# Two edits in the odd layer of a decoder trunk: normed heads without their softmax sums, and a mask added on another engine

## The chip, the core and the metric

The kernel runs on one core of a Trainium2 chip. A core has a tensor engine (TensorE, PE in the profile) whose weight loads (PEld) run ahead of its matmuls, a vector engine (VectorE, DVE), a scalar engine (ScalarE, ACT), GpSimd (POOL), and SyncE (SP), which here issues nearly all DMAs. Each engine takes its instructions in order and waits for the others by semaphores. Matmuls write to PSUM; the other data lie in SBUF. The metric is device time in microseconds (us), the median of several runs.

## The reference

Two layers on 1024 tokens of width 1024. The odd layer runs four differential heads (two attention maps, one subtracted from the other, then an RMS norm over the head's 128 outputs) beside eight forgetting heads (a causal softmax with a bias per key):

```python
def rmsnorm(x, g):
    y = x * lax.rsqrt(jnp.mean(x * x, axis=-1, keepdims=True) + NORM_EPS)
    return y * g

def diff_attention(q1, q2, k1, k2, v, lam):          # per block of 128 queries
    p = softmax(s1, axis=-1) - lam * softmax(s2, axis=-1)
    return einsum('bhqk,bkhe->bqhe', p, v)

def forgetting_attention(q, k, v, fcum):
    s = einsum('bqhd,bkhd->bhqk', q, k) * scale
    s = s + fcum[query] - fcum[key]
    s = where(causal_mask, s, -1e30)
    return einsum('bhqk,bkhd->bqhd', softmax(s, axis=-1), v)

o_d = rmsnorm(diff_attention(...), subln) * (1.0 - lam_init)
o = concatenate([o_d, forgetting_attention(...)]) * silu(z_gate)
return o @ w_out
```

## The kernel before

Activations lie with features on the 128 partitions and tokens along the free axis, in two halves of 512 tokens. Float32 accuracy comes from splitting each operand into a high and a low part, so a projection is three matmuls (L127, L128, L130). The odd layer's attention is woven with its projections: `weave` takes turns between the main work (attention of units 0 to 3, the differential heads, then 4 to 7, two forgetting heads each) and the filling work (projections of the next unit, and at the end the first half of the output product). A scheduler then orders each engine's instructions when the program is built; that order is fixed on the chip.

For each block `i` of 128 queries, `scores` writes a row of n = 128 (i + 1) scores into the one PSUM tile S of 1024 columns (L442). `soft` then makes one pass on VectorE (L464) that adds a bias or mask, scales, writes P and gives each query's minimum of the negated scores, read out by a second short instruction; ScalarE takes the exponential with that minimum as bias and the sum as by-product (L466). TensorE turns blocks of P (L501), the turned blocks are split into pt_h (ScalarE, L91) and pt_l (VectorE, L92), and the products with V follow (L510, L511, for differential heads L515 to L517) into a PSUM tile o.

The forgetting heads get their causal mask on TensorE: `scores` with `causal=True` closes each row with a bf16 product of an identity and the 128x128 mask (L446) into the row's last 128 columns. Their bias f, one row of 1024 keys broadcast to all partitions, is loaded per head by SP (L1009) into a tile x8 and added in `soft`.

In a differential head, P1 + (-lam l1 / l2) P2 is formed from the unnormalised maps (L945), so o is l1 times too large, where l1 is the first map's sum for each query. `to_rows` takes the reciprocals of four blocks' l1 (L475), transposes them on VectorE (L476), and writes them to memory in four small DMAs (L479); `step` loads them back broadcast (L958). `done` multiplies o by them on VectorE (L963) and squares the result on ScalarE (L964). `later` calls `rstd`, which sums the squares on TensorE (L205), adds EPS to the mean (L207), takes the reciprocal root by a bit trick and three Newton steps on VectorE, and spreads it again with TensorE (L217); L968 to L970 scale, gate (on GpSimd) and store.

GpSimd otherwise makes the low parts of weights (L92), which wait for ScalarE's high parts, the rope products (L348), the gates' share of the forgetting heads' sums (L492), and clears small tiles for `to_rows` (L474). Temporary tiles of 128x512 share eight buffers under the tag `t`.

Of the kernel before, what the change touches and what calls it, by code (L numbers as in the profile page):

```python
# [21 lines left out]
EPS = 1e-6  # L22
# [11 lines left out]
class Trunk:  # L34
# [161 lines left out]

    def rstd(self, s, n, col=None):
# [43 lines left out]
    def setup2(self):  # L241
# [7 lines left out]
        nc.vector.tensor_copy(self.smask, tri[:, :256])  # L249
        self.identb = self.const("identb", [128, 128], BF16)  # L250
        nc.vector.tensor_copy(self.identb, self.ident)
        self.nsink = self.const("nsink", [128, 8])
# [173 lines left out]

    def scores(self, qs, ks, i, keys, S, causal=False):

# [6 lines left out]
        while k0 < k1:  # L435
# [3 lines left out]
            dst = S[:, o:o + w]  # L439
            more = causal and e == k1  # L440
            for n, (a, k) in enumerate(zip(q, ks[k0 // 4])):
                nc.tensor.matmul(dst, a, k[:, s], start=(n == 0), stop=(n == len(q) - 1 and not more))  # L442
            o += w
            k0 = e
            if more:
                nc.tensor.matmul(S[:, o - 128:o], self.identb, self.mask[:, 896:], start=False, stop=True)  # L446

# [12 lines left out]
    def soft(self, S, n, add, scale, P, l, init=BIG):  # L460

        nc = self.nc
        nm = self.small()
        nc.vector.tensor_tensor_reduce(out=P[:, :n], in0=S[:, :n], in1=add, scale=-scale, scalar=init,  # L464
                                       op0=ALU.add, op1=ALU.min, accum_out=nm)
        nc.scalar.activation(P[:, :n], P[:, :n], AF.Exp, bias=nm, scale=-1.0, accum_out=l)  # L466
# [455 lines left out]
    def diff_items(self, u, st):  # L922
        nc = self.nc
        for c in range(2):
            o, L, steps = [], self.small(4), []
            for j in (2 * c, 2 * c + 1):
# [3 lines left out]

                def s_op(e, i, m, c=c, Ps=Ps, maps=maps, S_=S_, P_=P_, L=L, steps=steps):
                    n = 128 * (i + 1)
# [8 lines left out]
                    else:  # L941
# [19 lines left out]
                def done(c=c, o=o, steps=steps):  # L961
                    z, s = self.tmp(), self.tmp()
                    nc.vector.tensor_tensor(out=z, in0=o[0], in1=steps[0], op=ALU.mult)  # L963
                    nc.scalar.activation(s, z, AF.Square)  # L964

                    def later():
                        r = self.rstd(s, 128)
                        nc.vector.scalar_tensor_tensor(out=z, in0=z, scalar=self.subl, in1=r, op0=ALU.mult, op1=ALU.mult)  # L968
# [6 lines left out]
                        for e, i in enumerate((2 * j, 2 * j + 1)) for m in range(2)],  # L975
                       self.causal_groups(j, Ps, get, self.pv128, 0.162, lambda: st["V"], 0, step if j % 2 else None),
                       done if j % 2 else None, 1, 1 / 16.5)
# [25 lines left out]
    def forget_items(self, u, st):  # L1003
# [7 lines left out]
        for c in range(2):  # L1011
            for hh in range(2):
                def scores(i, S, hh=hh):
                    self.scores([a[hh] for a in st["q"][:i // 4 + 1]], [a[hh] for a in st["k"][:i // 4 + 1]], i,
                                (0, i + 1), causal=True, S=S)

                def done(o, c=c, hh=hh):
                    self.finish64(o, hh, st["g"][c], (1, u, c))
                    return ("mark", "odd0") if (u, c, hh) == (7, 0, 1) else None

                yield from self.causal_items(c, hh, scores, 0.108, lambda n, f=fb[hh]: f[:, :n], SC64, lambda: st["V"], done,
                                             1 / 26, (1, u, c), st["g"][c])
# [415 lines left out]
```

## Time and profile before

| | |
|---|---|
| median of 3 runs | 1376.84 us (1373.97 to 1377.67) |
| the profiled execution | 1375.71 us |
| its span, first to last instruction | 1373.9 us |
| mean granted TensorE clock | 0.989 |
| the first 690 us (the even layer and what lies before it) | TensorE busy 628.4 us, VectorE 490.9, ScalarE 381.1, GpSimd 185.8 |
| 715 to 860 us (most of the differential heads) | TensorE busy 135.9 of 145 us |

A row of a group reads: line, engine, operation, tile written <- tiles read, shapes, count | busy us, mean ns of one | idle us of the engine just before, and what ended it. A row of the timeline reads: start, duration, the instruction, and in brackets idle time before it. The durations of matmuls are modelled to their end and overlap, so two starts tell more of TensorE's pace than one duration. In names, `S` is the score tile, `p` the softmax numerators, `pj` a projection's sum, `wr` a raw weight and `wh`, `wl` its parts, `sm` small columns of statistics, `x` (x8) the bias f, `t` a temporary.

### The profile page before, as it was taken

The numbers are of one execution on the slowest core, as the hardware profiler recorded it, in microseconds if no ns is written. First come the engines' busy times: TensorE is split into PE (matmuls) and PEld (weight loads), VectorE is DVE, ScalarE is ACT, GpSimd is POOL, SyncE is SP. The second block draws the span as 40 slices with busy tenths as digits, with TensorE's granted clock in tenths as the row PEclk, the third lists the DMA queues.
The fourth block names the chain that finished last, engine by engine and source line by source line (L and its number), as shares of the span: only waits on it lengthen the run. The fifth ranks groups of instructions, "written<-read, shape, count | busy, mean of one in ns | idle before, by whom it ended". The sixth has DMA issues, their size and how long they took to land.

```text
span 1373.9 us, 20797 instructions
## 1 busy us (share of the span) xinstructions
PE 1274.9 (93%) x6940; PEld 1056.0 (77%) x6940; DVE 905.0 (66%) x1963; ACT 732.0 (53%) x1507; POOL 333.4 (24%) x316
## 2 busy tenths in 40 slices
PE   2899999999999999899889999999999999999996
PEld 1678778888777777778767777787888888887885
DVE  5855767777767775787877775767645554555475
ACT  4253226666457677854546554546445555556642
POOL 2243421421332215300103232321212111113400
PEclk9899999999999999999999999999999999999998
DMA  8706685555444543472623221212212121233283
GB/s 281 250 17 211 201 274 190 171 171 157 127 151 135 162 131 116 131 230 100 194 87 94 77 80 54 70 51 86 62 35 81 49 76 54 85 108 116 77 268 116
DMA packets 105132, 175.98 MB, mean 128 GB/s; under 512 B 16688, under 2 KB 25904, under 8 KB 105024
## 3 DMA queue, kind: packets, MB, share of 16 engines
q1 hardware_dynamic: 100512, 172.03, 39.5%
q10 hardware_dynamic: 4512, 2.62, 0.6%
q8 instruction: 54, 0.88, 0.3%
q14 instruction: 54, 0.44, 0.1%
HBM read 131.45 MB, written 31.74 MB: 119 GB/s over the span
## 4 chain that ended last, share of the span: by engine, by line
PE 54%; DVE 19%; DMA 9%; issue 8%; ACT 7%; SPq 2%; POOL 1%; DVEq 0%; POOLq 0%; ACTq 0%
PE pj L127 9%; PE pj L128 9%; PE pj L130 9%; PE S L442 7%; PE pt L501 4%; PE o L511 2%; DMA wr<-in_wout_dram 2%; DVE p L464 2%; PE S L127 2%; PE o L510 2%; PE S L130 2%; PE S L128 2%; DVE pt_l L92 2%; ACT p L466 1%; DVE t L347 1%
## 5 line engine op out<-in xcount | busy, mean ns | idle before, releaser
L127 PE MATMUL pj<-h,wh 128*128 128x512 f32 (+1 forms) x816 | 341.0, 418 | 2.0 <-ACT wh L91 2.0
L128 PE MATMUL pj<-h,wh 128*128 128x512 f32 (+1 forms) x816 | 322.2, 395 | 0.0
L130 PE MATMUL pj<-h,wl 128*128 128x512 f32 (+1 forms) x800 | 315.9, 395 | 1.6 <-DVE wl L92 1.6
L92 POOL TENSOR_TENSOR wl<-wr,wh 128x512 fp32r<-128x512 f32 x126 | 165.4, 1322 | 473.6 <-ACT wh L91 429.0
L466 ACT ACTIVATE p<-p,sm 128x128 f32<-128x128 f32 (+3 forms) x192 | 148.8, 775 | 140.4 <-DVE sm L464 137.9
L92 DVE TENSOR_TENSOR pt_l<-pt,pt_h 128x512 fp32r<-128x512 f32 (+1 forms) x232 | 147.0, 635 | 107.7 <-ACT pt_h L91 106.0
L442 PE MATMUL S<-qk,qk 96*128 96x512 f32 (+5 forms) x720 | 174.7, 344 | 21.5 <-DVE sm L464 12.4
L91 ACT ACTIVATE pt_h<-pt 128x512 fp32r<-128x512 f32 (+1 forms) x232 | 127.7, 552 | 100.3 <-PE pt L501 97.2
L130 PEld LDWEIGHTS pj<-h,wl 128*128 128x128 f32 x800 | 151.0, 189 | 34.0 <-DVE wl L92 3.1
L127 PEld LDWEIGHTS pj<-h,wh 128*128 128x128 f32 (+1 forms) x816 | 154.3, 189 | 20.1 <-ACT wh L91 2.9
L442 PEld LDWEIGHTS S<-qk,qk 128*128 128x128 f32 (+1 forms) x720 | 120.6, 189 | 63.4 <-DVE sm L464 27.7
L128 PEld LDWEIGHTS pj<-h,wh 128*128 128x128 f32 (+1 forms) x816 | 154.3, 189 | 16.6 <-DVE h L92 0.2
L91 ACT ACTIVATE wh<-wr 128x512 fp32r<-128x512 f32 x165 | 101.3, 622 | 118.4 <-PE S L128 38.7
L501 PE MATMUL pt<-ident,p 128*128 128x128 f32 x840 | 134.3, 275 | 3.7 <-DVE p L945 2.8
L501 PEld LDWEIGHTS pt<-ident,p 128*128 128x128 f32 x840 | 101.1, 140 | 27.0 <-DVE p L945 4.4
L464 DVE CUSTOM_DVE_ANT_0 p<-S,mask 128x640 f32<-128x640 f32 (+7 forms) x128 | 96.0, 750 | 33.8 <-PE S L442 33.0
L510 PE MATMUL o<-pt_h,v 128*128 128x256 f32 (+1 forms) x408 | 106.6, 281 | 1.5 <-ACT pt_h L91 1.0
L511 PE MATMUL o<-pt_l,v 128*128 128x256 f32 (+1 forms) x408 | 102.6, 286 | 5.5 <-DVE pt_l L92 5.1
L348 POOL TENSOR_TENSOR t<-t,rs 128x512 f32<-128x512 f32 x26 | 36.5, 1402 | 238.5 <-DMA t<-t 159.6
L511 PEld LDWEIGHTS o<-pt_l,v 128*128 128x128 f32 x408 | 77.3, 189 | 15.7 <-DVE pt_l L92 10.3
L510 PEld LDWEIGHTS o<-pt_h,v 128*128 128x128 f32 x408 | 77.2, 189 | 9.6 <-ACT pt_h L91 3.4
L464 DVE CUSTOM_DVE_ANT_0 p<-S,x 128x128 f32<-128x128 f32 (+3 forms) x64 | 48.2, 753 | 25.2 <-PE S L446 21.9
(315 smaller groups left out, 2284.7 us busy)
## 6 DMA issues: line engine op xcount, KB each, us to landing
wr<-in_wod_dram SPq DMA_DIRECT2D x80, 256.0 KB
wr<-in_wout_dram SPq DMA_DIRECT2D x68, 256.0 KB
ad<-in_wadab_dram SPq DMA_DIRECT2D x41, 256.0 KB
wr<-in_wev_dram SPq DMA_DIRECT2D x38, 256.0 KB
raw<-in_wadaa_dram SPq DMA_DIRECT2D x32, 256.0 KB
ogd<-t SPq DMA_DIRECT2D x32, 256.0 KB
t<-t SPq DMA_DIRECT2D x106, 64.0 KB
t<-rd SPq DMA_DIRECT2D x48, 128.0 KB
```

What stands on the lines that cost most here:

```text
L91: nc.scalar.activation(hi, src, AF.Copy)
L92: (lo_eng or nc.vector).tensor_tensor(out=lo, in0=src, in1=hi.bitcast(F32), op=ALU.subtract)
L127: nc.tensor.matmul(p, w[0][:, k, :m], h[0], start=first, stop=False)
L128: nc.tensor.matmul(p, w[0][:, k, :m], h[1], start=False, stop=last and w[1] is None)
L130: nc.tensor.matmul(p, w[1][:, k, :m], h[0], start=False, stop=last)
L348: nc.gpsimd.tensor_tensor(out=s, in0=s, in1=self.rs[:, cs], op=ALU.mult)
L442: nc.tensor.matmul(dst, a, k[:, s], start=(n == 0), stop=(n == len(q) - 1 and not more))
L464: nc.vector.tensor_tensor_reduce(out=P[:, :n], in0=S[:, :n], in1=add, scale=-scale, scalar=init, op0=ALU.add, op1=ALU.min, accum_out=nm)
L466: nc.scalar.activation(P[:, :n], P[:, :n], AF.Exp, bias=nm, scale=-1.0, accum_out=l)
L501: nc.tensor.transpose(pt[:, n * 128:n * 128 + 128], b, self.ident)
L510: nc.tensor.matmul(o[:, qcols], w, hi[:, cols], start=start, stop=False)
L511: nc.tensor.matmul(o[:, qcols], w, lo[:, cols], start=False, stop=stop)
```

## The change

Two edits. First, a differential head's o stays unnormalised: with o' = l1 o, the norm o / sqrt(mean(o^2) + EPS) equals o' / sqrt(mean(o'^2) + EPS l1^2), so `rstd` takes EPS l1^2 (one small operation on the column of sums) in place of EPS, and `to_rows`, its DMAs and the multiplication of o go. ScalarE copies o out of PSUM and squares it. Second, the mask product goes; for each forgetting head and half GpSimd adds the mask to the 512 bias columns of that half's diagonal blocks (a tile W of tag `t`), and `soft` makes two passes: the first n - 128 columns with f, then the last 128 with W, starting from the first pass's minimum.

```diff
-        nc.vector.tensor_scalar(v, p[:, :nb], 1.0 / n, EPS, op0=ALU.mult, op1=ALU.add)
+        if eps is None:
+            nc.vector.tensor_scalar(v, p[:, :nb], 1.0 / n, EPS, op0=ALU.mult, op1=ALU.add)
+        else:
+            nc.vector.scalar_tensor_tensor(out=v, in0=p[:, :nb], scalar=1.0 / n, in1=eps, op0=ALU.mult, op1=ALU.add)
...
-            if more:
-                nc.tensor.matmul(S[:, o - 128:o], self.identb, self.mask[:, 896:], start=False, stop=True)
...
-        nm = self.small()
-        nc.vector.tensor_tensor_reduce(out=P[:, :n], in0=S[:, :n], in1=add, scale=-scale, scalar=init,
-                                       op0=ALU.add, op1=ALU.min, accum_out=nm)
+        k = 0
+        for a in add if isinstance(add, list) else [add]:
+            nm, s = self.small(), slice(k, k + a.shape[-1])
+            nc.vector.tensor_tensor_reduce(out=P[:, s], in0=S[:, s], in1=a, scale=-scale, scalar=init,
+                                           op0=ALU.add, op1=ALU.min, accum_out=nm)
+            init, k = nm, s.stop
...
-                        if i % 4 == 3:
-                            self.to_rows(L, self.rd[1, u, c, 0])
...
-                def step(c=c, steps=steps):
-                    t = self.tmp()
-                    nc.sync.dma_start(t, self.rd[1, u, c, 0:1, :].to_broadcast([128, C]))
-                    steps.append(t)
...
-                    nc.vector.tensor_tensor(out=z, in0=o[0], in1=steps[0], op=ALU.mult)
-                    nc.scalar.activation(s, z, AF.Square)
+                    nc.scalar.activation(z, o[0], AF.Copy)
+                    nc.scalar.activation(s, o[0], AF.Square)
+                    nc.vector.scalar_tensor_tensor(out=L, in0=L, scalar=EPS, in1=L, op0=ALU.mult, op1=ALU.mult)
...
-                        r = self.rstd(s, 128)
+                        r = self.rstd(s, 128, eps=L)
...
+                W = self.tmp()
+                tri = self.mask[:, 896:].rearrange("p (o k) -> p o k", o=1).to_broadcast([128, 4, 128])
+                nc.gpsimd.tensor_tensor(out=W.rearrange("p (b k) -> p b k", b=4), in1=tri, op=ALU.add,
+                                        in0=fb[hh][:, c * C:c * C + C].rearrange("p (b k) -> p b k", b=4))
+
+                def add(n, f=fb[hh], W=W, c=c):
+                    d = W[:, n - 128 - c * C:n - c * C]
+                    return [f[:, :n - 128], d] if n > 128 else d
...
-                                (0, i + 1), causal=True, S=S)
+                                (0, i + 1), S=S)
```

The order changes from the first differential head's finish on. Line numbers after the change are shifted by up to four in the code before `forget_items`; L463 is L464 of before, L441 is L442.

TensorE in unit 4, second half, first head (block 4, 640 columns: a 512-wide and a 128-wide piece of S). Before:

```order
L442 MATMUL S_10567<-qk_9919,qk_9730 128x128
L501 MATMUL pt_10556<-ident,p_10426 128x128 x3
L442 MATMUL S_10567<-qk_6995,qk_9730 128x128
L446 LDWEIGHTS identb
L446 MATMUL S_10567<-mask,identb 128x128
L127 MATMUL pj_10536<-h_7243,wh_10241 128x512
L128 MATMUL pj_10536<-h_7244,wh_10241 128x512
```

After:

```order
L441 MATMUL S_10503<-qk_9853,qk_9673 128x128
L441 MATMUL S_10503<-qk_6993,qk_9673 128x128
L127 MATMUL pj_10470<-h_7241,wh_10168 128x512
L501 MATMUL pt_10492<-ident,p_10357 128x128 x3
L128 MATMUL pj_10470<-h_7242,wh_10168 128x512
```

The load of the identity and the mask product are gone, and three turns moved behind the score row.

VectorE at the same place, the softmax of blocks 4 and 5. Before:

```order
L92 TENSOR_TENSOR pt_l_10545<-pt_10540,pt_h_10544 128x384
L464 ISA p_10568,sm_10574<-S_10567,x_2172_10215 128x640
L464 ISA sm_10574 128x1
L92 TENSOR_TENSOR pt_l_10561<-pt_10556,pt_h_10560 128x384
L464 ISA p_10584,sm_10590<-S_10583,x_2172_10215 128x768
L464 ISA sm_10590 128x1
```

After:

```order
L463 ISA p_10504,sm_10509<-S_10503,x_2157_10142 128x512
L463 ISA sm_10509 128x1
L92 TENSOR_TENSOR pt_l_10479<-pt_10474,pt_h_10478 128x384
L92 TENSOR_TENSOR pt_l_10497<-pt_10492,pt_h_10496 128x384
L463 ISA p_10504,sm_10511<-S_10503,t_10489,sm_10509 128x128
L463 ISA sm_10511 128x1
L463 ISA p_10521,sm_10526<-S_10520,x_2157_10142 128x640
L463 ISA sm_10526 128x1
L463 ISA p_10521,sm_10528<-S_10520,t_10489,sm_10526 128x128
L463 ISA sm_10528 128x1
```

Each pass is now two, the second with W (here `t_10489`) and the first one's minimum; in block 4 two pt_l splits stand between them, in block 5 nothing.

GpSimd at the start of unit 7, the last pair of forgetting heads. Before:

```order
L92 TENSOR_TENSOR wl_12854<-wr_12855,wh_12853 128x512
L92 TENSOR_TENSOR wl_12854<-wr_12859,wh_12853 128x512
L92 TENSOR_TENSOR wl_12864<-wr_12865,wh_12863 128x512
L474 MEMSET t_12566 128x32
L474 MEMSET t_12699 128x32
L92 TENSOR_TENSOR wl_12864<-wr_12869,wh_12863 128x512
L492 TENSOR_TENSOR g_11708<-g_11708,t_12526 128x512
```

After:

```order
L92 TENSOR_TENSOR wl_12857<-wr_12858,wh_12856 128x512
L92 TENSOR_TENSOR wl_12857<-wr_12862,wh_12856 128x512
L1010 TENSOR_TENSOR t_12455<-x_2681_12451,mask 128x512
L92 TENSOR_TENSOR wl_12867<-wr_12868,wh_12866 128x512
L92 TENSOR_TENSOR wl_12867<-wr_12872,wh_12866 128x512
L474 MEMSET t_12556 128x32
L1010 TENSOR_TENSOR t_12593<-x_2682_12453,mask 128x512
L474 MEMSET t_12693 128x32
L1010 TENSOR_TENSOR t_12718<-x_2681_12451,mask 128x512
L492 TENSOR_TENSOR g_11674<-g_11674,t_12514 128x512
```

The tables W (L1010) stand between the weight splits: the first head's behind one pair, the second head's (`x_2682`) behind the next pair and a memset.

More of the change, by code (lines that the diff above doesn't have):

```diff
@@ L195, in squares, with rstd @@
         return acc
-    def rstd(self, s, n, col=None):
+    def rstd(self, s, n, col=None, eps=None):
         nc = self.nc
@@ L249, in setup2 @@
         nc.vector.tensor_copy(self.smask, tri[:, :256])
-        self.identb = self.const("identb", [128, 128], BF16)
-        nc.vector.tensor_copy(self.identb, self.ident)
         self.nsink = self.const("nsink", [128, 8])
@@ L425, in stack_k, with scores @@
         return out
-    def scores(self, qs, ks, i, keys, S, causal=False):
+    def scores(self, qs, ks, i, keys, S):
         nc = self.nc
@@ L439, in scores @@
             dst = S[:, o:o + w]
-            more = causal and e == k1
             for n, (a, k) in enumerate(zip(q, ks[k0 // 4])):
-                nc.tensor.matmul(dst, a, k[:, s], start=(n == 0), stop=(n == len(q) - 1 and not more))
+                nc.tensor.matmul(dst, a, k[:, s], start=(n == 0), stop=n == len(q) - 1)
             o += w
             k0 = e
-            if more:
-                nc.tensor.matmul(S[:, o - 128:o], self.identb, self.mask[:, 896:], start=False, stop=True)
     def room(self, alloc, j, share=0):
@@ L924, in diff_items @@
         for c in range(2):
-            o, L, steps = [], self.small(4), []
+            o, L = [], self.small(4)
             for j in (2 * c, 2 * c + 1):
@@ L929, in diff_items, with s_op @@
                           for f, s in ((lambda: self.psum("S"), 0), (lambda: self.t("p", [128, 1024]), 2)))
-                def s_op(e, i, m, c=c, Ps=Ps, maps=maps, S_=S_, P_=P_, L=L, steps=steps):
+                def s_op(e, i, m, c=c, Ps=Ps, maps=maps, S_=S_, P_=P_, L=L):
                     n = 128 * (i + 1)
@@ L954, in get, with done @@
                     return o[0][:, jj * 256:jj * 256 + 256]
-                def step(c=c, steps=steps):
-                    t = self.tmp()
-                    nc.sync.dma_start(t, self.rd[1, u, c, 0:1, :].to_broadcast([128, C]))
-                    steps.append(t)
-                def done(c=c, o=o, steps=steps):
+                def done(c=c, o=o, L=L):
                     z, s = self.tmp(), self.tmp()
-                    nc.vector.tensor_tensor(out=z, in0=o[0], in1=steps[0], op=ALU.mult)
-                    nc.scalar.activation(s, z, AF.Square)
+                    nc.scalar.activation(z, o[0], AF.Copy)
+                    nc.scalar.activation(s, o[0], AF.Square)
+                    nc.vector.scalar_tensor_tensor(out=L, in0=L, scalar=EPS, in1=L, op0=ALU.mult, op1=ALU.mult)
                     def later():
-                        r = self.rstd(s, 128)
+                        r = self.rstd(s, 128, eps=L)
                         nc.vector.scalar_tensor_tensor(out=z, in0=z, scalar=self.subl, in1=r, op0=ALU.mult, op1=ALU.mult)
@@ L975, in diff_items @@
                         for e, i in enumerate((2 * j, 2 * j + 1)) for m in range(2)],
-                       self.causal_groups(j, Ps, get, self.pv128, 0.162, lambda: st["V"], 0, step if j % 2 else None),
+                       self.causal_groups(j, Ps, get, self.pv128, 0.162, lambda: st["V"], 0),
                        done if j % 2 else None, 1, 1 / 16.5)
@@ L1019, in done @@
                     return ("mark", "odd0") if (u, c, hh) == (7, 0, 1) else None
-                yield from self.causal_items(c, hh, scores, 0.108, lambda n, f=fb[hh]: f[:, :n], SC64, lambda: st["V"], done,
+                yield from self.causal_items(c, hh, scores, 0.108, add, SC64, lambda: st["V"], done,
                                              1 / 26, (1, u, c), st["g"][c])
```

## The prediction

> **What bounds the kernel now.** I read the page first, then the busy times by stage, then the waits of the stage that the change touches most.
>
> ```profile
> span 1373.9 us, 20797 instructions
> ...
> PE 1274.9 (93%) x6940; PEld 1056.0 (77%) x6940; DVE 905.0 (66%) x1963; ACT 732.0 (53%) x1507; POOL 333.4 (24%) x316
> ```
>
> TensorE is busy for 93% of the span, but that is a mean over stages with different limits. The change touches only the odd layer's attention. In the next table the columns are each engine's busy time in us (and instructions), the granted clock, the DMA share and GB/s:
>
> ```profile
> 690.00:860.00 170.00, 154.14 (x793) 125.43 (x792) 116.30 (x261) 84.14 (x170) 43.38 (x36) 0.99 0.26 78
> 860.00:1000.00 140.00, 136.44 (x723) 112.18 (x723) 96.11 (x221) 72.25 (x138) 32.21 (x28) 1.00 0.22 66
> 1000.00:1290.00 290.00, 287.02 (x1626) 237.58 (x1625) 149.72 (x325) 159.74 (x327) 62.28 (x63) 1.00 0.24 77
> 1290.00:1374.00 84.00, 68.84 (x506) 63.68 (x504) 51.99 (x127) 34.80 (x74) 9.68 (x9) 0.94 0.52 171
> ```
>
> From about 715 to 1000 us the differential heads run; TensorE is not busy for 15.9 us of the first row and 3.6 us of the second. From 1000 to 1290 us the forgetting heads run, and there TensorE is busy for 287.0 of 290 us at full clock, VectorE for half, GpSimd for a fifth. So in the forget stage **TensorE's own work sets the time**: an instruction taken from it is worth its length there, and work for VectorE or GpSimd costs nothing until TensorE waits for it. How near that is, the waits of the forget stage say (us, times, longest):
>
> ```profile
> DVE p L464 <- PE S L446: 21.9, 26, 5.8
> ...
> PEld S L442 <- DVE sm L464: 4.4, 10, 0.9
> ...
> PE S L442 <- DVE sm L464: 1.1, 3, 0.5
> ```
>
> In 10 of the 64 score rows a product (L442) had to wait for the softmax (L464) to leave the one S buffer, as seen by the weight loads, and 1.1 us of it reached the matmuls. VectorE came too early for its scores 26 times.
>
> **The mask products go.** The trace has 64 of them:
>
> ```profile
> L446 PE MATMUL S<-mask,identb 128*128 128x128 bf16 x64 | 14.7, 230 | 0.0
> ```
>
> Their 230 ns are not their price, since matmuls overlap. The price is how much later the next ones start. Here are a 256-wide score product with its mask product and the projection after it, then a 256-wide product without a mask; then the same for 128 columns. The first number is the start.
>
> ```profile
> 1122.01 0.28 PE L442 MATMUL S<-ad,qk 128*128 128x256 f32 x1
> 1122.13 0.23 PE L446 MATMUL S<-mask,identb 128*128 128x128 bf16 x1
> 1122.17 0.48 PE L127 MATMUL pj<-h,wh 128*128 128x512 f32 x1
> 1122.48 0.39 PE L128 MATMUL pj<-h,wh 128*128 128x512 f32 x1
> ...
> 1123.31 0.28 PE L511 MATMUL o<-pt_l,v 128*128 128x256 f32 x1
> 1123.42 0.40 PE L127 MATMUL pj<-h,wh 128*128 128x512 f32 x1
> 1123.66 0.40 PE L128 MATMUL pj<-h,wh 128*128 128x512 f32 x1
> ```
> ```profile
> 1102.62 0.28 PE L442 MATMUL S<-ad,qk 128*128 128x128 f32 x1
> 1102.73 0.23 PE L446 MATMUL S<-mask,identb 128*128 128x128 bf16 x1
> 1102.77 0.48 PE L127 MATMUL pj<-h,wh 128*128 128x512 f32 x1
> 1103.09 0.39 PE L128 MATMUL pj<-h,wh 128*128 128x512 f32 x1
> ```
> ```profile
> 1001.36 0.28 PE L517 MATMUL o<-pt_h,v 128*128 128x128 f32 x1
> 1001.47 0.44 PE L127 MATMUL pj<-h,wh 128*128 128x512 f32 x1
> 1001.76 0.39 PE L128 MATMUL pj<-h,wh 128*128 128x512 f32 x1
> ```
>
> From the start of the last product before to the start of L128 it takes 0.47 us with the mask and 0.35 without, so 0.12; behind a 128-wide product 0.47 and 0.40, so 0.07. Most of it is not the mask's own 0.04 us but the slower start of the next product (0.31 instead of 0.23 to its successor). A score row ends in a piece of 128 columns in one of four blocks. For wider pieces I take the 256-wide price: 16 x 0.07 + 48 x 0.12 = **-6.9 us**. The ends are 64 x 0.04 = 2.6 and 64 x 0.23 = 14.7.
>
> The Trainium skill, "TensorE: Matmul & The Clock Gate", section "Back-to-back issue gap", gives about 81 ns for each pair of weight load and 128-column matmul in a sustained stream; by it, an estimate, 64 go for 5.2 us. The rows above give 0.07 to 0.12 us, so the measured price stands.
>
> **The softmax is split on VectorE.** A forget row of n columns was one reduction over S plus f; now it is one over the first n - 128 columns and one over the diagonal 128 that starts from the first one's minimum, for 7 of 8 blocks of each of 8 heads, 56 in all.
>
> ```profile
> L464 DVE CUSTOM_DVE_ANT_0 p<-S,x 128x640 f32<-128x640 f32 x8 | 6.6, 819 | 0.7 <-PE S L446 0.5
> ...
> L464 DVE CUSTOM_DVE_ANT_0 p<-S,x 128x512 f32<-128x512 f32 x8 | 5.5, 689 | 2.9 <-PE S L446 2.9
> ...
> L464 DVE DVE_READ_ACCUMULATOR2_ANT sm<- 128x1 f32 x64 | 5.3, 82 | 0.0
> ...
> L464 DVE CUSTOM_DVE_ANT_0 p<-S,x 128x128 f32<-128x128 f32 x8 | 2.3, 282 | 0.0
> ```
>
> 689 + 282 + 82 - 819 = 234 ns more each, 13.1 us in all. At the other end the second reduction is added whole, 282 + 82 = 364 ns: 20.4 us. Beside 150 of 290 us that is room enough, so it costs only where TensorE waits for S. Behind a split softmax stand, on VectorE, the next pt_l split and the next softmax; for these wait the exponential on ScalarE, the P·V products and the next scores. Of the 10 waits each grows by 0.23, less the 0.07 us by which S is ready earlier (mask product's end 1122.36, score product's end 1122.29): 10 x 0.16 = **+1.6 us**, which I take; the ends are 0 and 56 x 0.36 = 20.4. The order shows one thing more: in 24 of the 56 the compiler's scheduler set something between the two halves, 14 times a pt_l split, which waits for ScalarE.
>
> **The tables on GpSimd.** Sixteen additions of 128x512 join its queue, one for each head and half. Each wants its f row, loaded on SP's queue, and stands behind weight splits that wait for ScalarE. The tightest place in the order is unit 7, second head, behind two weight splits and a memset:
>
> ```profile
> 1224.97 1.28 POOL L92 TENSOR_TENSOR wl<-wr,wh 128x512 fp32r<-128x512 f32 x1 [10.00 <-ACT wh L91]
> 1226.19 0.18 POOL L474 MEMSET t<- 128x32 f32 x2
> 1226.33 1.28 POOL L92 TENSOR_TENSOR wl<-wr,wh 128x512 fp32r<-128x512 f32 x1
> ```
> ```profile
> 1234.88 0.28 DVE L464 CUSTOM_DVE_ANT_0 p<-S,x 128x128 f32<-128x128 f32 x1
> ```
>
> The table would be ready at 1227.61 + 1.3 = 1228.9, and its softmax ran at 1234.88: 6 us of cover, hence **0**. If that cover went, each late table would hold up VectorE's whole queue by up to its 1.3 us, 16 x 1.3 = 21 us. From below it is also nothing, since GpSimd is on nobody's way here.
>
> **The differential heads.** Eight times (four heads, two halves) the reciprocal sums no longer travel: a memset, a reciprocal, a transpose, four small stores and one broadcast load go, 40 DMA issues from SP's queue. On VectorE the scaling of o goes too:
>
> ```profile
> L963 DVE TENSOR_TENSOR t<-o,t 128x512 f32<-128x512 f32 x8 | 5.5, 683 | 0.2
> ...
> L964 ACT ACTIVATE t<-t 128x512 f32<-128x512 f32 x8 | 5.0, 631 | 6.5 <-DVE t L963 6.3
> L476 DVE STREAM_TRANSPOSE t<-t 128x32 f32<-128x32 f32 x9 | 1.9, 211 | 0.2
> L475 DVE RECIPROCAL t<-sm 128x4 f32<-128x4 f32 x9 | 1.6, 173 | 0.6 <-ACT p L466 0.6
> ```
>
> VectorE loses 683 + 211 + 173 and gains one 128x4 operation for eps times l squared, by L475's row 173: 894 ns x 8 = 7.2 us. ScalarE gains a copy of o at 631 ns: 5.0 us. The way from o to its square stays as long (copy and square instead of product and square, 1.26 against 1.31 us), but no longer stands in VectorE's queue. What of that reaches TensorE is what it waits for the softmax in this stage, 715 to 1000 us:
>
> ```profile
> PE S L442 <- DVE sm L464: 6.8, 8, 2.4
> ```
>
> All of it could go (-6.8). At the other end, the four finishes before 860 us each put their ScalarE copy in the way of an exponential (+2.5). Nearest is the share of VectorE's work that goes: 7.2 of 116 + 96 us is 3%, which alone gives next to nothing, but the relief falls at the heads' ends where rope and softmax queue up, and the rope's ScalarE copies come earlier in the order, as their buffers are free sooner. I take a quarter, **-1.7 us**. The removed identity copy at the start runs once, beside loads: 0.
>
> **The sum.** -6.9 + 1.6 + 0 - 1.7 = -7.0 us. The end (1290 to 1374 us) is no longer TensorE's alone (68.8 of 84 us, DMA share 0.52), but all of it follows the attention, so it moves along. The profiled execution took 1375.7 us (span 1373.9), 1.1 below the median of three, 1376.84; from the median it is 1376.84 - 7.0 = **1369.8**.
>
> **Rivals.** (1) The S buffer takes the gain back. The 26 places where VectorE waited for scores are places where the softmax follows directly; if each also holds TensorE by its 0.23, that is +6.1 instead of +1.6: 1374.3, within 0.3%. For it speaks that S has one buffer; against it that only 10 waits are seen, with projections set between. 17%. (2) **Slower**: the softmax becomes the bound. If all 56 splits are exposed whole, 0.36 each, +20.4 replaces +1.6: 1388.6. It decides from 6.9 / 56 = 0.12 us exposed per split, at the S products of the heads' second halves (L442). For it speak the pt_l splits between the halves; against it VectorE's idle half. 8%. The Trainium skill, "VectorE: DVE Perf Modes", section "Rules for kernel authors", says to keep the number of VectorE operations small, since each one drains before the next; that speaks for this rival. The rows agree that a split costs more than its columns, 234 ns, but not that it is exposed. (3) The change doesn't do what it says: all 64 mask products and all 40 DMAs are gone from the order, so 0.
>
> **Numbers.** Forecast 75%, rival 1 17%, rival 2 8%. 0.3% (4.1 us) is about what a measurement of this kernel can tell from no change: faster 0.75, same 0.17, slower 0.08. Low end: the differential term whole (-6.8), the splits hidden: 1376.84 - 13.7 = 1363.1. High end: rival 1 with no gain in the differential heads, 1376.0. Rival 2 and some beyond the ends are left out.
>
> **What would show it.** The stage from 1000 to about 1283 us should hold the same work with TensorE still over 97% busy and no identb rows. "PE S <- DVE sm" waits there should stay under some 4 us; over 10 us means rival 2. VectorE's busy time there should rise by 13 to 20 us and its waits name L442, not GpSimd; a wait "DVE p <- POOL t" would make the table's term wrong. In the differential stage TensorE's idle time should shrink by 1 to 3 us; if it grows, the ScalarE copy is in the way.

## The result and the profile after

The changed kernel took 1366.43 us (median of 6 runs, 1363.14 to 1368.67) against 1376.07 us for the kernel before (6 runs): ratio 0.9925, 95% interval 0.9909 to 0.9941, which is 10.3 us less (8.1 to 12.5). Timed a second time, beside other experiments, it took 1366.29 us against 1373.8: 0.9938 (0.9918 to 0.9957), 8.5 us less. (The two pairs of medians themselves lie 9.6 and 7.5 us apart; a change of the whole time in us is worked out from the ratio here and below.) The forecast was 7.0 us less and 1369.8 us; direction, range and most of the size hold. Whether its steps hold is another matter.

Span and busy times of the page after, then the stages with the windows cut about where the same work ends (columns as before: us, PE, PEld, DVE, ACT, POOL, clock, DMA share, GB/s):

```profile
span 1366.9 us, 20727 instructions
...
PE 1269.7 (93%) x6876; PEld 1055.4 (77%) x6876; DVE 912.3 (67%) x2058; ACT 734.4 (54%) x1515; POOL 352.5 (26%) x324
```
```profile
690.00:860.00 170.00, 157.46 (x810) 129.15 (x809) 116.65 (x257) 87.50 (x176) 45.18 (x32) 0.98 0.24 72
860.00:998.00 138.00, 135.39 (x716) 111.08 (x715) 92.62 (x212) 73.64 (x141) 31.77 (x25) 1.00 0.20 59
998.00:1284.00 286.00, 281.45 (x1561) 236.06 (x1560) 159.84 (x436) 158.66 (x327) 79.97 (x79) 1.00 0.24 78
```

In the first row TensorE is not busy for 12.5 us instead of 15.9, in the second for 2.6 instead of 3.6: the differential heads wait less. In the forget stage it is the other way round, 4.6 of 286 us instead of 3.0 of 290: there TensorE has less to do, but waits more. VectorE's work there grew by 10 us and GpSimd's by 18; between the two instructions that bound the stage below, it is 16 and 18. The waits of TensorE after (us, times, longest), first in the differential stage (713 to 998 us):

```profile
PE S L441 <- DVE sm L463: 4.1, 5, 1.9
```

and in the forget stage (998 to 1284 us):

```profile
PE S L441 <- DVE sm L463: 2.6, 7, 0.8
...
PEld S L441 <- DVE sm L463: 4.0, 10, 1.1
...
DVE p L463 <- PE S L441: 17.0, 19, 5.6
```

Before, these were 6.8 in the first and 1.1, 4.4 and 21.9 us in the second. No row says that VectorE's softmax waits for GpSimd. The new work of the forget stage (line, engine, operation, tiles, shapes, count | busy us, mean ns; one of the 16 tables lies before the window):

```profile
L463 DVE CUSTOM_DVE_ANT_0 p<-S,t,sm 128x128 f32<-128x128 f32 x56 | 19.5, 347 | 1.5
...
L1010 POOL TENSOR_TENSOR t<-x,mask 128x512 f32<-128x512 f32 x15 | 18.3, 1221 | 4.1 <-DMA rd<-t 4.1
```

A whole time scatters by several us from run to run, but the same instruction can be found in each trace, and the time between two of them is far steadier. I use three: the first exponential of the differential heads, the first of the forgetting heads, and the last turning of P (L501). The first two, before and then after (start, duration):

```profile
731.28 0.39 ACT L466 ACTIVATE p<-p,sm 128x128 f32<-128x128 f32 x1
...
1002.18 0.40 ACT L466 ACTIVATE p<-p,sm 128x128 f32<-128x128 f32 x1 [0.62 <-DVE sm L464]
```
```profile
734.12 0.39 ACT L466 ACTIVATE p<-p,sm 128x128 f32<-128x128 f32 x1
...
1000.07 0.40 ACT L466 ACTIVATE p<-p,sm 128x128 f32<-128x128 f32 x1 [0.69 <-DVE sm L463]
```

So the **differential stage** took 270.90 us before and 265.95 after, -4.95. The **forget stage**, from there to the last L501, took 297.47 us before and 293.52 after, -3.95. The second profile of the changed kernel gives -3.19 and -4.31. Forecast were -1.7 and -5.3. The remaining 74 us differ from before by -2.6 to +1.8 us among these kernels, ten below and three above; the granted clock falls to 0.50 there in every profile, for 7 to 17 us in all.

The granted clock matters in the differential stage too. In the forget stage it is 1.00 throughout in all 14 profiles. In the differential stage it is so in some; in others it falls to 0.50 once or twice, for about 3.4 us each time. Here are two profiles of the changed kernel at the same place of its program, the second with such a fall (the clock is the third number from the end):

```profile
809.00:814.00 5.00, 5.00 (x28) 4.26 (x29) 2.91 (x7) 2.30 (x5) 1.29 (x1) 1.00 0.11 26
```
```profile
806.00:811.00 5.00, 5.00 (x22) 4.13 (x21) 2.55 (x6) 2.14 (x5) 1.28 (x1) 0.66 0.09 23
```

TensorE waits 1.9 us for the softmax just before, in both. The second profile then loses 1.2 us on the first by the clock, and another 0.6 near 880 us whose cause stays open. All profiles, in us against before, with the number of such falls in the differential stage (before had none):

| kernel | edit | differential | falls of the clock | forget |
|---|---|---|---|---|
| changed kernel, two profiles | both | -4.95, -3.19 | 0, 1 | -3.95, -4.31 |
| e1_norm_only | norm alone | -3.52 | 1 | -0.08 |
| e5_norm_rows_kept | norm, way of the sums kept | -3.59 | 0 | -0.02 |
| e6_norm_vector_copy | norm, o copied by VectorE | -2.03 | 1 | +0.06 |
| e10_norm_load_kept | norm, the broadcast load kept | +0.15 | 2 | -0.22 |
| e2_mask_only | mask alone | -0.22 | 0 | -3.76 |
| e3_split_only | the two reductions alone | -0.09 | 0 | +1.55 |
| e4_no_mask | mask products and mask left out | -0.83 | 0 | -6.77 |
| e9_no_mask_split | mask left out, two reductions | -0.49 | 0 | -4.97 |
| b1_one_pass_restore | both, one reduction, VectorE copies | -3.32 | 1 | -4.03 |
| b2_one_pass_scalar | both, one reduction, ScalarE copies | -4.94 | 0 | -5.33 |
| b3_tables_vector | both, tables on VectorE | -3.85 | 1 | -5.14 |

Where an edit does not touch a stage, the forget stage repeats to 0.2 us and the differential stage to 0.8; the changed kernel's own two profiles differ by 0.4 and 1.8. That is the resolution of what follows, and in the differential stage only profiles with as many falls of the clock compare well. All ratios are to the kernel before on the same chip, with 95% intervals.

### The profile page after: what moved, and what is told of

It reads as the page before. It is cut to its first block, busy times and chain, and to the rows that moved or that the text cites. A ratio compares the mean times of both kernels' runs of the same rounds, so it can differ in the third digit from the quotient of the medians.

```text
span 1366.9 us, 20727 instructions
## 1 busy us (share of the span) xinstructions
PE 1269.7 (93%) x6876; PEld 1055.4 (77%) x6876; DVE 912.3 (67%) x2058; ACT 734.4 (54%) x1515; POOL 352.5 (26%) x324
## 4 chain that ended last, share of the span: by engine, by line
PE 42%; DVE 12%; ACT 6%; issue 5%; DMA 5%; POOL 1%; SPq 1%; POOLq 0%; DVEq 0%; ACTq 0%
PE pj L127 8%; PE pj L128 8%; PE pj L130 8%; PE S L441 6%; PE pt L501 3%; PE o L511 2%; DVE pt_l L92 1%; DVE p L463 1%; DMA wr<-in_wout_dram 1%; PE o L510 1%; ACT wh L91 1%; PE S L127 1%; PE S L130 1%; PE S L128 1%; DMA t<-wd 1%
## 5 line engine op out<-in xcount | busy, mean ns | idle before, releaser
L441 PE MATMUL S<-qk,qk 96*128 96x512 f32 (+5 forms) x720 | 175.3, 344 | 20.6 <-DVE sm L463 11.4
L441 PEld LDWEIGHTS S<-qk,qk 128*128 128x128 f32 (+1 forms) x720 | 120.2, 188 | 63.2 <-DVE sm L463 25.5
L501 PE MATMUL pt<-ident,p 128*128 128x128 f32 x840 | 134.3, 274 | 3.1 <-DVE p L945 3.1
L501 PEld LDWEIGHTS pt<-ident,p 128*128 128x128 f32 x840 | 101.5, 140 | 26.1 <-DVE p L945 4.4
L463 DVE CUSTOM_DVE_ANT_0 p<-S,mask 128x640 f32<-128x640 f32 (+7 forms) x128 | 96.0, 750 | 35.0 <-PE S L441 34.1
L348 POOL TENSOR_TENSOR t<-t,rs 128x512 f32<-128x512 f32 x26 | 36.8, 1414 | 229.0 <-DMA t<-t 147.4
L127 PE MATMUL S<-h,wh 128*128 128x512 f32 (+1 forms) x144 | 57.5, 399 | 3.9 <-ACT h L332 2.7
```

Of the source, the lines that this page charges most:

```text
L127: nc.tensor.matmul(p, w[0][:, k, :m], h[0], start=first, stop=False)
L348: nc.gpsimd.tensor_tensor(out=s, in0=s, in1=self.rs[:, cs], op=ALU.mult)
L441: nc.tensor.matmul(dst, a, k[:, s], start=(n == 0), stop=n == len(q) - 1)
L463: nc.vector.tensor_tensor_reduce(out=P[:, s], in0=S[:, s], in1=a, scale=-scale, scalar=init, op0=ALU.add, op1=ALU.min, accum_out=nm)
L501: nc.tensor.transpose(pt[:, n * 128:n * 128 + 128], b, self.ident)
```

## The experiments

**e1_norm_only and e2_mask_only: one edit each.** The two halves of the diff above, each on the kernel before:

```diff
-  nc.vector.tensor_tensor(out=z, in0=o[0], in1=steps[0], op=ALU.mult)
-  nc.scalar.activation(s, z, AF.Square)
+  nc.scalar.activation(z, o[0], AF.Copy)
+  nc.scalar.activation(s, o[0], AF.Square)
```

> The kernel before with the first edit alone (differential heads normed without division; mask products stay on TensorE, softmax in one pass). By the prediction's terms: -1.7 us, about 1374.4 (ratio 0.9988). By the landmarks of the two profiled runs, which gained 4.9 us between 731 and 1000 us: -4.9 us or somewhat more, ratio about 0.9964, with the idle time of TensorE from 715 to 1000 us down by about 4 us and the softmax waits of the S products (6.8 us before) near 4. If the gain of that stage was luck of one execution or came from the second edit: within 0.1% of before.

Measured: 0.9967 (0.9952 to 0.9981), -4.5 us; -3.52 in the differential stage, nothing in the forget stage. The gain of that stage is the first edit's, and about twice the forecast, with one fall of the clock in it. Its waits, from 728 to 1000 us:

```profile
PE S L444 <- DVE sm L466: 4.3, 5, 1.9
```

In the same window of the kernel before there stand also:

```profile
PE pt L205 <- ACT t L964: 1.0, 2, 0.5
PE pt L501 <- DVE v L92: 0.9, 1, 0.9
```

The wait for the softmax, 6.8 us before, shrinks by 2.5; the wait of the norm's sums for the square (1.0) and one of the value split (0.9) are gone. The forecast counted only the first.

```diff
-  (0, i + 1), causal=True, S=S)
+  (0, i + 1), S=S)
+  W = self.tmp()
+  nc.gpsimd.tensor_tensor(out=W..., in1=tri, op=ALU.add, in0=fb[hh]...)
```

> The kernel before with the second edit alone (mask tables on GpSimd, softmax of a forget row in two passes; the differential heads are normed as before). By the prediction's terms: -6.9 + 1.6 = -5.3 us, ratio 0.9961, all of it between 1000 and 1290 us. By the landmarks of the two profiled runs: -3.9 us, ratio 0.9972. By rival 1 (the S buffer takes the gain back): -0.8 us, ratio 0.9994. If the two edits add up, e1_norm_only and e2_mask_only together give the 9.6 us of the whole change.

Measured: 0.9977 (0.9964 to 0.9991), -3.2 us, and -3.76 in the forget stage. The edits add up in the traces (-3.5 and -3.8 against -3.2 to -5.0 and -4.0 to -4.3 together), and in the times within their intervals. So the mask edit gave less than its -5.3, and the question is which of its terms.

**e3_split_only and e4_no_mask: one term each.**

```diff
-  lambda n, f=fb[hh]: f[:, :n], SC64, ...
+  lambda n, f=fb[hh]: [f[:, :n - 128], f[:, n - 128:n]] if n > 128 else f[:, :n], SC64, ...
```

> The kernel before with only the softmax of the forgetting heads split into the two reductions; the mask products stay on TensorE and no table is built on GpSimd. It prices the split alone. By the prediction's term: +1.6 us (ratio 1.0012). By rival 1: +6.1 us (1.0044). By rival 2: up to +20.4 us (1.0148). If the forget stage gave less than predicted because the split costs more than 1.6: about +3. If it gave less because the mask products were worth less: +1.6 or less here, and e4_no_mask shows less than 6.9.

Measured: 1.0014 (0.9998 to 1.0029), +1.55 us in the forget stage. The forecast's +1.6 for the split holds, although its working was off: the 64 softmax operations and their read-outs take 48.2 + 5.3 us before, the 120 after the change 60.2 + 9.9, which is 296 ns more for each of the 56 splits instead of 234, because the second reduction, which starts from a column (p<-S,t,sm), takes 347 ns and not 282. Rivals 1 and 2 (+6.1, +20.4) fall.

```diff
-  (0, i + 1), causal=True, S=S)
+  (0, i + 1), S=S)
```

> The kernel before with the 64 mask products left out and nothing in their place, so the forgetting heads' scores above the diagonal are not masked: this part of the computation is left out, while the amount of all other work is the same. It prices the mask products on TensorE alone. By the prediction's term: -6.9 us (ratio 0.9950); by the low end, 0.04 us each: -2.6 us (0.9981); by their whole 230 ns each: -14.7 us (0.9893). The S buffer is also free some 0.07 us earlier at each row, which may add up to 1 us to it.

Measured: 0.9958 (0.9939 to 0.9977), -6.77 us in the forget stage, in a kernel that leaves the causal mask of these heads out. The sum of the forecast comes out; the rows' own 230 ns would have been more than twice too much. By units of 16 products (from the first exponential of one to that of the next) the gain is 1.40, 1.40, 1.18 and 2.79 us. Units 4 to 6 give 0.083 us for each product, inside the 0.07 to 0.12 read from the starts of neighbours, and at that rate 64 are worth 5.3 us. Unit 7 gave 1.5 more. In that unit of the kernel before, VectorE's split of h into its two parts runs beside GpSimd's gate product and takes 1.73 us:

```profile
1227.68 1.73 DVE L92 TENSOR_TENSOR h<-h,h 128x512 fp32r<-128x512 f32 x1
```
```profile
1227.57 1.29 POOL L492 TENSOR_TENSOR g<-g,t 128x512 f32<-128x512 f32 x1
```

In e4_no_mask, whose order differs, no split of h takes more than 0.69. How much of the 1.5 us this makes is not shown. And -6.77 + 1.55 = -5.2, and the mask edit gave -3.8 to -4.3: about 1 us is missing, and the only part not yet tried is the tables on GpSimd.

**e9_no_mask_split: mask products out, softmax split, no tables.** It is e3 and e4 together.

> The kernel before without the 64 mask products and with the softmax of the forgetting heads in two reductions, but with no tables on GpSimd: the causal mask of the forgetting heads is left out, all other work of the mask edit is there. From 1002 to 1299 us e4_no_mask gained 6.8 us, e3_split_only lost 1.5 and e2_mask_only gained 3.8, so 1.5 are missing in the sum. Theory I, the split costs more once TensorE is faster: -3.8 us in that stretch, as e2_mask_only (ratio about 0.997). Theory T, the tables on GpSimd cost it (VectorE's operations beside GpSimd's become longer, or a late table): -5.2 us (ratio about 0.996).

Measured: 0.9969 (0.9955 to 0.9984), -4.97 us in the forget stage. So the split costs 1.8 with the mask products gone, nearly all of it in units 6 and 7 (1.1 and 0.8), and the tables cost the rest: 1.0 us by the mean of the three profiles that have them (-3.76, -3.95, -4.31). In e2_mask_only the order of TensorE, VectorE and ScalarE is the same as here without the tables, and 1.04 of the 1.2 us between the two come up in unit 7. VectorE there without the tables:

```profile
1234.11 0.69 DVE L92 TENSOR_TENSOR pt_l<-pt,pt_h 128x512 fp32r<-128x512 f32 x1
1234.72 0.68 DVE L92 TENSOR_TENSOR h<-h,h 128x512 fp32r<-128x512 f32 x1
1235.32 0.69 DVE L557 TENSOR_TENSOR t<-t,g 128x512 f32<-128x512 f32 x1
```

and the same rows in e2_mask_only, with what GpSimd does meanwhile:

```profile
1232.22 0.69 DVE L92 TENSOR_TENSOR pt_l<-pt,pt_h 128x512 fp32r<-128x512 f32 x1
1232.82 1.49 DVE L92 TENSOR_TENSOR h<-h,h 128x512 fp32r<-128x512 f32 x1
1234.24 0.68 DVE L552 TENSOR_TENSOR t<-t,g 128x512 f32<-128x512 f32 x1
```
```profile
1232.61 1.16 POOL L1013 TENSOR_TENSOR t<-x,mask 128x512 f32<-128x512 f32 x1 [4.14 <-DMA rd<-t]
```

The table was not late; it ran. While it ran, VectorE's split of h, whose two inputs both lie in SBUF, took 1.49 us instead of 0.68, and the softmax behind it came later by that much. Of VectorE's 438 operations in the stage only three are over 0.05 us longer with the tables, splits of h each beside a table: this one, one of 0.93 us at 1222.00, and one of 1.30 at 1210.81, which did not delay TensorE. The group of that split (8 in the stage) without the tables and with them:

```profile
L92 DVE TENSOR_TENSOR h<-h,h 128x512 fp32r<-128x512 f32 x8 | 5.5, 691 | 1.8 <-ACT h L91 1.7
```
```profile
L92 DVE TENSOR_TENSOR h<-h,h 128x512 fp32r<-128x512 f32 x8 | 7.2, 896 | 2.2 <-ACT h L91 2.2
```

The operations with an input in PSUM (pt_l, the softmax) keep their length. No wait shows any of this: the time is inside the busy time of VectorE's instruction.

**b3_tables_vector: the tables on VectorE.** The changed kernel with one word changed:

```diff
-  nc.gpsimd.tensor_tensor(out=W..., in1=tri, op=ALU.add, in0=fb[hh]...)
+  nc.vector.tensor_tensor(out=W..., in1=tri, op=ALU.add, in0=fb[hh]...)
```

> The changed kernel with its 16 mask tables added by VectorE instead of GpSimd: 16 operations of 128x512 on VectorE, 0.69 us each by its rows of that size, 11 us more work on it, and nothing of the change is left on GpSimd. From 1002 to 1299 us the changed kernel gained 3.9 and 4.3 us in its two profiles, e9_no_mask_split (no tables at all) 5.0. If what the tables cost is that VectorE's split of h runs 0.9 to 1.5 us instead of 0.69 beside them: those splits come back to 0.69 us and the stretch gains 4.5 to 5 us (ratio about 0.993). If VectorE's added 11 us hold up the softmax instead: less than 3.9 there, with longer waits of the S products for the softmax than the 2.6 us of the changed kernel.

Measured: 0.9936 (0.9914 to 0.9957); -5.14 us in the forget stage, as without any tables. The h splits are back to 0.69 us, and 11 us of added work on VectorE (this row has 14 of the 16) cost nothing that shows. TensorE's order changed as well in this kernel, so it agrees with the cause but doesn't show it alone:

```profile
L1010 DVE TENSOR_TENSOR t<-x,mask 128x512 f32<-128x512 f32 x14 | 9.7, 705 | 0.0
...
L92 DVE TENSOR_TENSOR h<-h,h 128x512 fp32r<-128x512 f32 x8 | 5.5, 688 | 1.5 <-ACT h L91 1.3
```

**b1_one_pass_restore: no split at all.** The diagonal blocks are masked among adjoining columns, so that one reduction does, and after each row VectorE puts the clean block back; GpSimd copies the second halves' clean columns.

```diff
+  if c:
+      nc.gpsimd.tensor_copy(W, half)
+      nc.gpsimd.tensor_tensor(out=four(half), in0=four(W), in1=tri, op=ALU.add)
...
+  def behind(i, f=f, W=W, c=c):
+      if i % 4 < 3:
+          a, b = f[:, i * 128:i * 128 + 128], W[:, i % 4 * 128:i % 4 * 128 + 128]
+          nc.vector.tensor_copy(a if c else b, b if c else a)
```

> The changed kernel with the softmax of a forget row in one reduction again: the diagonal blocks are masked by GpSimd in one table of adjoining columns, and after each row VectorE copies the clean block back over the masked one (48 copies of 128x128, an estimate of 130 to 200 ns each by the 128-wide rows of VectorE, behind the release of S). GpSimd gets 8 copies of 128x512 more. If the two reductions are what the forget stage gave back (theory I): from 1002 to 1299 us -6 to -6.8 us against before, some 2.5 better than the changed kernel, and about -12 in all (ratio 0.991). If the tables on GpSimd are (theory T): no better than the changed kernel, -3 to -4 in that stretch.

Measured: 0.9931 (0.9912 to 0.9949), but only -4.03 us in the forget stage, no better than the changed kernel. VectorE's copies, and GpSimd at the first of them:

```profile
1014.46 1.17 DVE L1022 COPY t<-x 128x128 f32<-128x128 f32 x1
...
1016.24 0.23 DVE L1022 COPY t<-x 128x128 f32<-128x128 f32 x1
```
```profile
1014.38 1.16 POOL L1012 TENSOR_TENSOR x<-t,mask 128x512 f32<-128x512 f32 x1
```

The same copy takes 0.23 us alone and 1.17 beside GpSimd: it ends at 1015.63, 0.09 after GpSimd's operation. The 48 copies took 18.3 us (means of 413 and 344 ns for the two directions), not the 6 to 10 that I had estimated. Whether this is what ate the gain of the one reduction, the next kernel tests.

**b2_one_pass_scalar: ScalarE puts the block back.** The second halves' clean columns come by DMA.

```diff
-  nc.gpsimd.tensor_copy(W, half)
+  nc.sync.dma_start(W, self.fd[hd:hd + 1, C:].to_broadcast([128, C]))
...
-  nc.vector.tensor_copy(a if c else b, b if c else a)
+  nc.scalar.activation(a if c else b, b if c else a, AF.Copy)
```

> As b1_one_pass_restore, but ScalarE copies the clean blocks back (48 copies of 128x128) and the second halves' clean copies are loaded by DMA instead of copied by GpSimd. In b1_one_pass_restore VectorE's copies took 227 ns where GpSimd was idle and up to 1.36 us beside its operations, 18.3 us in all, and the stretch from 1002 to 1299 us gained 4.0 us. If that contention is what ate the gain of the one reduction: -5 to -6 us there against before, ratio about 0.991. If the one reduction needs its restored block too soon whichever engine brings it (the softmax then waits for ScalarE): -4 or less, with waits of the softmax (L461) for ScalarE in the trace.

Measured: 0.9931 (0.9918 to 0.9944); -5.33 us in the forget stage, 1.3 better than b1_one_pass_restore by its copies and the second halves' clean columns alone. Part of the rest goes into a new wait of the softmax:

```profile
DVE p L461 <- ACT x L1023: 8.3, 8, 1.4
DVE p L461 <- ACT t L1023: 4.9, 9, 1.0
```

In the forget stage b2 and b3 beat the changed kernel by about 1 us. Their whole times (1364.72 and 1364.42 us) do not tell them from it: the intervals overlap almost wholly.

**e6, e5 and e10: which part of the norm edit.** Each is e1_norm_only with one thing put back. In e6 VectorE copies o, an operation of the removed one's size:

```diff
-  nc.scalar.activation(z, o[0], AF.Copy)
+  nc.vector.tensor_copy(z, o[0])
```

> The first edit alone, as in e1_norm_only, but o is copied out of PSUM by VectorE instead of ScalarE: VectorE gets an operation of about the removed one's size (683 ns, 8 times) back and ScalarE loses its new one, while the way of the reciprocal sums (memset, reciprocal, transpose, stores, broadcast load, its buffer) stays gone. Theory 1, the scaling in VectorE's queue was what cost: most of e1_norm_only's -4.5 us is lost, about -1 remains (ratio 0.9993). Theory 2, the way of the sums with its buffer and queue slots was what cost: about -4.5 stays (0.9967). The wait of the rstd products for ScalarE (L205 before, 1.0 us) should come back under theory 1 only.

Measured: 0.9984 (0.9971 to 0.9998), -2.03 us in the differential stage: between the two theories. Its waits of TensorE, 728 to 1000 us:

```profile
PE S L444 <- DVE sm L466: 4.2, 5, 2.1
...
PE pt L503 <- DVE v L92: 0.9, 1, 0.9
...
PE pt L204 <- ACT t L960: 0.5, 1, 0.5
```

The wait of 0.9 us for the value split and half of that for the square came back; that for the softmax stayed at 4.2. So the length of the operation on VectorE is worth 1.5 us beside e1_norm_only (the clock fell once in both), and 2.0 go with the sums' way or with what its absence does to the order.

In e5 the reciprocal, its transpose, the stores and the load all stay; only a store of 64 numbers reads what is loaded:

```diff
+  if i % 4 == 3:
+      self.to_rows(L, self.rd[1, u, c, 0])
...
+  def step(c=c):
+      t = self.tmp()
+      nc.sync.dma_start(t, self.rd[1, u, c, 0:1, :].to_broadcast([128, C]))
+      nc.sync.dma_start(self.wd[0, c, 0:1, :64], t[0:1, :64])
```

> The first edit alone, but the way of the reciprocal sums is kept without use: per head and half the memset, reciprocal, transpose, four small stores and the broadcast load into its 128x512 buffer stay, and one store of 64 numbers reads that buffer. VectorE only loses the scaling of o (683 ns, 8 times). From 731 to 1002 us e1_norm_only gained 3.5 us and e6_norm_vector_copy, with the scaling's size put back on VectorE, 2.0. If the parts add up, 1.5 us is the scaling's and 2.0 the way's: this one gains 1.5 there, ratio about 0.998. If the scaling in the queue needs nothing else to go, it gains 3.5 as e1_norm_only (0.9967).

Measured: 0.9972 (0.9959 to 0.9984), -3.59 us, as much as e1_norm_only. But the clock fell once in e1_norm_only and not here. Beside the two profiles of the whole edit without a fall (-4.95 and -4.94), 1.3 us are missing. So most of the gain needs only that the scaling of o leaves VectorE, and the sums' way seems to cost something over 1 us beside it. By the same comparison e6, with one fall, stays 1.2 to 1.8 short of the four others with one (-3.19 to -3.85). These are single profiles, and the intervals of the whole times of e1, e5 and e6 overlap.

In e10 only the load and the store of 64 numbers stay:

```diff
-  if i % 4 == 3:
-      self.to_rows(L, self.rd[1, u, c, 0])
...
-  nc.sync.dma_start(t, self.rd[1, u, c, 0:1, :].to_broadcast([128, C]))
+  nc.sync.dma_start(t, self.rd[0, u, c, 0:1, :].to_broadcast([128, C]))
```

> As e5_norm_rows_kept, but only the broadcast load into a 128x512 buffer and the store of 64 numbers are kept (the load brings rows of the even layer, which nothing uses); memset, reciprocal, transpose and the four stores are gone. Theory Q, VectorE's queue holds up the softmax: it gains nearly what e1_norm_only does, 3 to 3.5 us from 731 to 1002 us, and e5_norm_rows_kept about 1.5. Theory R, the load's buffer and its wait hold back the rope's buffers: it gains no more than e5_norm_rows_kept. The rope's products (L347 and L349 before) should stand late beside GpSimd's work, 1 us or longer each near 750 us, where theory R holds.

Measured: 1.0 (0.9986 to 1.0014), no gain, though it does less than e5. Theory Q would have it gain 3 us; theory R, which wants it no better than e5, would have the rope late, and it was not:

```profile
743.96 0.68 DVE L349 TENSOR_TENSOR t<-t,rc 128x512 f32<-128x512 f32 x1
```

The only long product of the rope near there (1.18 us at 756.87) stands in e1_norm_only just the same. Up to 851 us it was 2.7 us ahead, and lost 2.4 between 860 and 913. There VectorE and GpSimd of e10:

```profile
880.02 0.75 DVE L970 SCALAR_TENSOR_TENSOR t<-t,subl,pt 128x512 f32<-128x512 f32 x1
880.69 0.21 DVE L945 SCALAR_TENSOR_TENSOR sm<-sm,nlam,sm 128x1 f32<-128x1 f32 x1
880.82 2.38 DVE L425 TENSOR_TENSOR ad<-t,qk 64x512 fp32r<-64x512 f32 x2
883.23 1.80 DVE L947 SCALAR_TENSOR_TENSOR p<-p,sm,p 128x640 f32<-128x640 f32 x1
884.95 0.95 DVE L466 CUSTOM_DVE_ANT_0 p<-S,mask 128x768 f32<-128x768 f32 x1
```
```profile
880.85 1.80 POOL L971 TENSOR_TENSOR t<-t,g 128x512 f32<-128x512 f32 x1 [2.13 <-DVE t L970]
882.62 1.73 POOL L92 TENSOR_TENSOR wl<-wr,wh 128x512 fp32r<-128x512 f32 x1
```

and the same operations of VectorE in e1_norm_only:

```profile
879.47 0.89 DVE L947 SCALAR_TENSOR_TENSOR p<-p,sm,p 128x640 f32<-128x640 f32 x1
880.27 1.40 DVE L425 TENSOR_TENSOR ad<-t,qk 64x512 fp32r<-64x512 f32 x2
881.70 0.75 DVE L965 SCALAR_TENSOR_TENSOR t<-t,subl,pt 128x512 f32<-128x512 f32 x1
882.36 0.95 DVE L466 CUSTOM_DVE_ANT_0 p<-S,mask 128x768 f32<-128x768 f32 x1
```

In e10 the norm's product (L970) stands ahead of the rope's last step (L425) and the map's difference (L947). It releases GpSimd's gate product at 880.85, and both run into it: 2.38 instead of 1.40 us and 1.80 instead of 0.89. The softmax behind them frees S late, and TensorE waits 1.86 us at that place. Right behind this wait the granted clock falls, for the second time in this profile:

```profile
886.00:891.00 5.00, 5.00 (x19) 4.24 (x20) 2.79 (x6) 2.00 (x4) 1.43 (x2) 0.66 0.36 118
```

Against e1_norm_only, e10 loses 3.4 us from 881 to 891 us: by size, the wait and the fall together. That the exchange made the wait is read from these rows and not tested. One exchange in VectorE's order, with the clock behind it, is worth as much as the effects that e5, e6 and e10 were to tell apart, so what the parts of the edit are worth separately stays open.

**a1_after_again: the changed kernel once more.**

> The changed kernel once more, beside the others on one chip. If its first timing holds: ratio 0.9925. If the two edits simply add up as e1_norm_only (0.9967) and e2_mask_only (0.9977) measured: 0.9944. In the trace: between 731 and 1002 us -3.5 to -5 us against before, from there to 1299 us -3.9.

Measured: 0.9938, -8.5 us; -3.19 and -4.31 us in the two stages. Between the first timing and the sum of the two edits (-7.7), and within the interval of either.

## Why the forecast came out near, point by point

- **"16 x 0.07 + 48 x 0.12 = -6.9"**: right in its sum, -6.8 in e4_no_mask, and in part by luck. Units 4 to 6 give 0.083 us for each product instead of the 0.107 of the forecast's mean; unit 7 made up for it, where a long split of h stood before. The starts of neighbours came near the price; the duration of 230 ns did not.
- **"10 x 0.16 = +1.6"**: right in size, +1.55 with the mask products and 1.8 without them, but not by its mechanism. After the change 10 weight loads still wait for the softmax, and for 4.0 us instead of 4.4: these waits did not grow. The waits that reach the matmuls rose from 1.1 to 2.6 us, and nearly all of the 1.8 us falls in units 6 and 7.
- **The tables, "0"**: wrong by 1.0 us. The step that failed is "From below it is also nothing, since GpSimd is on nobody's way here". No softmax waited for a table. But a table can stretch an operation of VectorE beside it whose inputs both lie in SBUF, as e2 against e9 shows. The trace of before had shown it, in the split of h above and in a rope product of 1.78 us with GpSimd's (L348) beside it, against 0.68 without:

```profile
750.60 1.78 DVE L347 TENSOR_TENSOR t<-t,rc 128x512 f32<-128x512 f32 x1
...
750.11 1.72 POOL L348 TENSOR_TENSOR t<-t,rs 128x512 f32<-128x512 f32 x1 [7.99 <-DMA t<-t]
```

- **The differential heads, "I take a quarter, -1.7"**: mis-sized. Six profiles of the five kernels with the whole norm edit show -3.2 to -5.0, mean -4.0: -4.9 where the clock did not fall, -3.2 to -3.8 where it fell once. In e1_norm_only, of the 6.8 us of softmax waits 2.5 went, a good third, and 1.9 us more came from two waits that the step left out. The reason given, VectorE's lighter queue, has e5 and e6 for it (most of the gain comes with the scaling alone, and putting its length back takes 1.5 away) and e10 against it, which has a lighter queue than e5 and gained nothing, with two falls of the clock. How the gain divides is not settled.
- **The sum**: the shortfall of 1.2 us in the forget stage and the surplus of 2.3 in the differential stage partly cancel. By the traces the two stages give -4.0 and -4.1, -8.1 together: inside the interval of the second timing and at the edge of the first, whose remaining 2 us no profile places. So the forecast of 7.0 came near partly because its misses had opposite signs.
- **What would show it**: TensorE stayed at 98% in the forget stage and its softmax waits at 2.6 us, under the 4 that were set, and VectorE's busy time there rose by 16 us, within the 13 to 20. In the differential stage TensorE's idle time shrank by 4.4 us (15.9 + 3.6 to 12.5 + 2.6), more than the 1 to 3 that were set. "DVE p <- POOL t" never came, and was the wrong thing to look for: the cost of the tables has no wait row.

## What to carry to other kernels

Before work is moved to GpSimd, look at what VectorE does at that time: here its operations with all inputs in SBUF could be held up until GpSimd's had ended, and the delay hid in busy time, where no list of waits names it. Price a removed matmul by the starts of its neighbours, and compare a change by the time between two instructions that both traces have: that resolved 0.2 to 0.4 us in the forget stage, where whole times resolved 2 to 3. Look at the granted clock of the stretch first: one fall of 3.4 us cost 1.2 us in the differential stage, as much as the parts that were to be told apart. And where a scheduler orders the engines, a variant that differs in one part may also differ in an exchange that is worth more than the part.

## What the runs showed of the hardware

In b1_one_pass_restore a VectorE copy of 128x128 within SBUF took 0.21 to 0.23 us with GpSimd idle and up to 1.35 beside one of its operations; at 1014.46 us it ended 0.09 us after GpSimd's. GpSimd is held as well: in e10 its gate product and weight split of 128x512 took 1.80 and 1.73 us instead of 1.29. The Trainium skill, "SBUF — State Buffer", section "SBUF: two separate sides", says that VectorE and GpSimd share one pair of SBUF ports by an exclusive lock, which on VectorE's side concerns operations in a two-port mode or, against a GpSimd operation that reads SBUF, with two SBUF inputs: whoever starts first holds it for the whole instruction, and the other is blocked. These rows agree, and so does it that VectorE's operations with an input in PSUM kept their lengths.

The granted clock fell to 0.50 for about 3.4 us behind waits of TensorE of 1.9 to 2.2 us in six of the nine profiles with the norm edit. Behind waits of 1.9 to 2.4 us in the same place it stayed at 1.00 in two others of the nine and in the five profiles without that edit, so the length of the wait alone does not settle it.
